# Two gate columns moved from plain products in the attention stage to a third seven-product unit in the recurrent stage

## The chip, the core and the metric

The program runs on one core of one Trainium2 chip, as a single launch. The metric is device time in microseconds (us). The engines are named as in the profile: PE (TensorE matmul), PEld (its weight load), DVE (VectorE), ACT (ScalarE), POOL (GpSimd) and SP (SyncE, which issues most of the DMAs).

## What is computed

The reference is one layer of a streaming encoder for 1024 prompt frames and 32 sample frames, of width 1024. What matters here is the first half of the layer: one input projection whose columns feed a windowed attention (A), a gated recurrence (B) and the two gates.

```python
h = _rms_norm(x, g_pre_mix)
z = h @ w_in
qa, ka, va, qb, fb, ib, ob, ga, gb = jnp.split(z, SPLIT_POINTS, axis=-1)
...
ya = _sink_attention(qblk, kblk, vblk, bias, mask, sinks)
yb, s_fin = _hgrn2(qb, fb, ib, s0, lb, block)
yb = _rms_norm(yb, g_hgrn_out) * jax.nn.silu(ob)
mix = jax.nn.sigmoid(ga) * (ya @ w_br_a) + jax.nn.sigmoid(gb) * (yb @ w_br_b)
x = x + _rms_norm(mix @ w_out, g_post_mix)
```

`ga` and `gb` are 1024 columns each. The kernel computes them in 16 blocks of 128 columns (called gate columns here, numbered 0 to 15 in the list `GATES`), takes their tanh and parks the result in DRAM until the branches are mixed.

## The kernel before

**Tokens and precision.** The 1056 frames lie across the free dimension in three groups of 384, 384 and 288 (`GR`). Each fp32 operand is held as a high part and a rest (`La`/`Lb` for the activations, `wh`/`wl` for a weight column, `wt` for both parts of a weight block), and each product is three matmuls: high by high, high by rest, rest by high.

**Plain columns.** `unit(out)` yields three blocks, one per token group. A block is 8 contraction steps of three matmuls, so 24 matmuls, issued in `product` (L205 to L207) in two halves of 12. One column is thus 72 matmuls. Its weights come through `load_next`: a DMA into a `wr` buffer, a cast on ACT (L184), and the rest either on DVE (L186) or, from the second attention pair on, by an ACT multiplication (L188) and an accumulating POOL DMA (L189). `gate_out` ends a gate block: tanh on ACT (L299), then a DMA to DRAM (L300).

**Attention stage.** Eight query columns hold two heads each ("pair" 0 to 7 here). For each pair nine score tiles are worked off: `scores` (PE L502 and L503, DVE L508, ACT L513, DVE L515 and L516, ACT L518), `turn` (PE transposes L539, then the split of the probabilities into `ph` on ACT L228 and `pl` on DVE L229) and `values` (PE L558 and L559, ACT L565, DVE L566 and L567). These small steps are put between the plain blocks of `blocks` by `stream`: those of pair `i` are spread over the three blocks of query column `i+1` and over `G_AT[i]` gate blocks. `G_AT` therefore says how many blocks of 24 matmuls stand beside each pair. Its sum over 3, `N_A`, is the number of gate columns done there. In pairs 1, 2, 4 and 5 `h_sums` adds sums of activations on DVE for the next stage (written to `t_d`).

**Between the stages.** One more plain gate column, `GATES[N_A]`, is streamed after the last pair, while the first weights of the next stage are prepared. The four sums are read back from `t_d` into `TL` (four DMAs, L991), and `t_split` makes `TH` (ACT L996) and the rest in `TL` (DVE L997).

**Recurrent stage.** Two weight columns at a time are multiplied by a Winograd form of Strassen's scheme: seven block products over the first two token groups (12 matmuls of 384 each), where plain products need eight, and four direct block products for the third group (12 matmuls of 288 each). `unit_pieces` (matmuls L1122, L1124, L1125) writes one such unit as 11 pieces. Its weights are loaded by `b_raw` (L1031) and summed and split by `b_parts` (L1043, L1044, L1049 to L1051, L1056). Each of the eight heads has two units, for (q, f) and (i, og). After the heads named in `G_AFTER`, a third unit holds two gate columns (`gate_unit`). `BU` lists all units in order; a unit's raw weights go to the two `wr` buffers or to two of the eight `wb` buffers in turn, counted from the end of `BU`, so that the last unit is in `wb`. The head's own work (`decay`, `factors`, `tile_in`, `tile_out`, `group_out`) is placed between the pieces by their number.

**After it.** Gate columns 14 and 15 are plain products again, and the branch products follow.

**Order.** What stands in the code is program order per step; a scheduler of the tile framework then fixes, at build time, one order per engine, and each engine works its own list in that order. `pinned` and `step` hold some steps behind others.

Of the kernel before, what the change touches and what calls it, by code (L numbers as in the profile page):

```python
# [59 lines left out]
def layer_kernel(  # L60
# [89 lines left out]

    plan = [in_cols(1024), in_cols(1152), in_cols(0)]
    GATES = [(ta_d[c], 5376 + c * P) for c in range(8)] + [(tb_d[c], 6400 + c * P) for c in range(8)]
    G_AT = (6,2,3,3,3,3,3,4)
    N_A = sum(G_AT) // 3
    plan_a = []
    for i in range(8):
        done, q = sum(G_AT[:i]), [("q", i + 1)] * (3 if i < 7 else 0)
        g = [("g", b // 3) for b in range(done, done + G_AT[i])]
        plan_a += g + q if i == 0 else q + g
# [120 lines left out]
    def unit(out):  # L280

        cell = []

        def get_w():
            if not cell:
                cell.append(next_w())
            return cell[0]
        return [(get_w, g, out) for g in range(3)]
# [6 lines left out]
    def gate_out(dst):  # L295
        def out(g, b):
            o, n = GR[g]
            t = gtile()
            S.activation(t[:, :n], b[:, :n], AF.Tanh, scale=0.5)  # L299
            dma(dst[:, o:o + n], t[:, :n])  # L300
        return out
# [17 lines left out]
    with right("ap") as ap:  # L319
# [93 lines left out]
        def q_out(i):  # L413
            def out(g, b):
                n = GR[g][1]
                qa = ap.tile([P, 384], F32R, tag="qa", name=nm("qa"), bufs=4)
                qb = ap.tile([P, 384], F32R, tag="qb", name=nm("qb"), bufs=4)
                if g == 2:
                    G.memset(qa[:, n + 32:384].bitcast(F32), 0.0)
                S.mul(qa[0:64, :n], b[0:64, :n], -0.125)  # L420
                V.scalar_tensor_tensor(qa[64:128, :n], b[0:64, :n], -0.125, qa[0:64, :n].bitcast(F32),
                                       op0=ALU.mult, op1=ALU.subtract)
                S.mul(qb[64:128, :n], b[64:128, :n], -0.125)
                V.scalar_tensor_tensor(qb[0:64, :n], b[64:128, :n], -0.125,
                                       qb[64:128, :n].bitcast(F32), op0=ALU.mult, op1=ALU.subtract)
                if g == 2:
                    G.tensor_copy(qa[:, n:n + 32], qb[:, SO:n].bitcast(F32))
                qs[i, g] = (qa, qb)
            return out
# [509 lines left out]
        for i in range(8):  # L939
            lo_ = 2 * len(blocks) if i else 0  # L940
            q = unit(q_out(i + 1)) if i < 7 else []
            g = [of_gates.pop(0) for _ in range(G_AT[i])]
            blocks += g + q if i == 0 else q + g
# [67 lines left out]
          5: (La[2][0:4], Lb[2][0:4]), 6: (La[2][4:8], Lb[2][4:8])}  # L1011


    G_AFTER = {3: N_A + 1, 7: N_A + 3}
    assert N_A + 5 == 14
    BU, unit_at = [], {}
    for h in range(8):
        unit_at[h] = len(BU)
        BU += [(1280 + h * P, 2304 + h * P), (3328 + h * P, 4352 + h * P)]
        if h in G_AFTER:  # L1020
            BU.append(tuple(GATES[G_AFTER[h] + a][1] for a in range(2)))
    NB = len(BU)
# [67 lines left out]
    with right("bp") as bp:  # L1090
# [121 lines left out]
        def gate_unit(h):  # L1212
            a, b = (gate_out(GATES[G_AFTER[h] + i][0]) for i in range(2))
            return unit_pieces(unit_at[h] + 2, lambda: gu, a,
                               lambda g: bt("x0", GMAX, 1)[:], b)
# [195 lines left out]
        for h in range(8):  # L1411
            m0 = len(pieces)
            pieces += qf_unit(h) + io_unit(h)
            m1 = m0 + NP
            if h in G_AFTER:
                pieces += gate_unit(h)
# [1510 lines left out]
def build(shapes):  # L2927
    import concourse.bacc as _bacc

    nc = _bacc.Bacc("TRN2", target_bir_lowering=False, num_devices=1)  # L2930
    args = [nc.dram_tensor(f"in_{n}_dram", s, F32, kind="ExternalInput").ap() for n, s in shapes]
    for i, shape in enumerate(_OUTS):
        args.append(nc.dram_tensor(f"out_{i}_dram", shape, F32, kind="ExternalOutput").ap())
    with tile.TileContext(nc) as tc:
        layer_kernel(tc, *args)
    return nc
# [10 lines left out]
```

## Time and profile before

| what | value |
|---|---|
| median of 3 runs | 1944.42 us (1942.07 to 1945.03) |
| the profiled execution | 1947.46 us |
| its span, first to last instruction | 1945.8 us |
| granted TensorE clock, mean over the span | 0.996 |
| busy share of the span | PE 99%, DVE 76%, ACT 53%, POOL 20% |
| attention pairs 1 to 7, with the column after them | about 112 us to 356 us of the span |
| recurrent stage | about 356 us to 825 us |

How to read it: "busy" is the time in which an instruction of the engine was under way, as the profiler models it. A matmul's own duration overlaps that of its neighbours, so the cost of a matmul in a dense stream is read from start to start, not from its duration. A row "X waited for Y" is idle time of engine X, and Y is what ended it. In a group's row, the last part is the idle time just before its instructions.

### The profile page before, as it was taken

How to read it: one execution, taken by the hardware profiler on the slowest of the kernel's cores; microseconds unless marked ns; L12 is line 12 of the kernel's file. 1: busy time of each engine (PE TensorE's matmuls, PEld its weight loads, DVE VectorE, ACT ScalarE, POOL GpSimd, SP SyncE). 2: the span in 40 equal slices, each digit the busy share in tenths (PEclk: the TensorE clock that was granted, in tenths of full speed). 3: DMA queues.
4: the chain of work that ended last, by engine and by line, in shares of the span. 5: the costliest groups of instructions: out<-in, count | busy, mean ns of one | idle time of the engine just before them, and what ended most of it. 6: DMA issues, size and time to landing. Idle time of an engine off the chain costs nothing.

```text
span 1945.8 us, 38169 instructions
## 1 busy us (share of the span) xinstructions
PE 1921.6 (99%) x14523; PEld 1903.9 (98%) x14523; DVE 1472.6 (76%) x3201; ACT 1028.7 (53%) x2214; POOL 381.4 (20%) x530
## 2 busy tenths in 40 slices
PE   8999999999999999999999999999999999999999
PEld 7999999999999999999999999999999999999998
DVE  5777777788888888755796878777787786768872
ACT  6667778666666666553445763333333336534432
POOL 2111211000101010132321113444644330000000
PEclk9999999999999999999999999999999999999999
DMA  8544443445547364498979684566897356755343
GB/s 267 150 111 129 127 131 90 149 114 139 146 106 162 118 122 101 129 312 272 293 203 296 230 280 131 161 171 188 158 187 183 115 186 215 220 178 159 117 131 88
DMA packets 319599, 329.11 MB, mean 169 GB/s; under 512 B 17432, under 2 KB 277435, under 8 KB 319416
## 3 DMA queue, kind: packets, MB, share of 16 engines
q1 hardware_dynamic: 274152, 218.92, 36.4%
q0 software_dynamic: 45136, 107.70, 23.1%
q8 instruction: 114, 1.87, 0.4%
q14 instruction: 69, 0.57, 0.1%
q10 hardware_dynamic: 128, 0.06, 0.0%
HBM read 234.48 MB, written 132.47 MB: 189 GB/s over the span
## 4 chain that ended last, share of the span: by engine, by line
PE 85%; DVE 6%; DMA 3%; ACT 3%; issue 2%; POOL 0%; SPq 0%; ACTq 0%; DVEq 0%; POOLq 0%
PE st L2373 7%; PE st L2372 7%; PE st L2371 7%; PE mm L205 4%; PE mm L206 4%; PE mm L207 4%; PE st L2499 4%; PE st L2501 4%; PE st L2500 4%; PE st L1663 2%; PE st L1665 2%; PE st L1667 2%; PE st L205 2%; PE st L206 2%; PE st L207 2%
## 5 line engine op out<-in xcount | busy, mean ns | idle before, releaser
L2373 PE MATMUL st<-op,wt 128*128 128x264 f32 x1232 | 349.9, 284 | 0.0
L2371 PE MATMUL st<-op,wt 128*128 128x264 f32 x1232 | 348.7, 283 | 1.2 <-ACT Sp L2383 0.5
L2372 PE MATMUL st<-op,wt 128*128 128x264 f32 x1232 | 347.8, 282 | 0.0
L2371 PEld LDWEIGHTS st<-op,wt 128*128 128x128 f32 x1232 | 231.3, 188 | 2.5 <-ACT Sp L2383 0.9
L2372 PEld LDWEIGHTS st<-op,wt 128*128 128x128 f32 x1232 | 231.5, 188 | 0.0
L2373 PEld LDWEIGHTS st<-op,wt 128*128 128x128 f32 x1232 | 230.9, 187 | 0.0
L2499 PE MATMUL st<-dop,wt 128*128 128x264 f32 x616 | 175.2, 285 | 2.6 <-ACT S L2514 2.6
L2501 PE MATMUL st<-dop,wt 128*128 128x264 f32 x616 | 175.0, 284 | 0.0
L2500 PE MATMUL st<-dop,wt 128*128 128x264 f32 x616 | 174.7, 284 | 0.0
L2030 ACT CAST wt<-wu 128x512 fp32r<-128x512 f32 x126 | 76.0, 618 | 176.4 <-POOL wu L2039 71.5
L205 PE MATMUL mm<-La,wh 128*128 128x384 f32 (+1 forms) x480 | 158.3, 330 | 0.0
L206 PE MATMUL mm<-Lb,wh 128*128 128x384 f32 (+1 forms) x480 | 155.2, 324 | 0.2 <-DVE Lb L784 0.2
L207 PE MATMUL mm<-La,wl 128*128 128x384 f32 (+1 forms) x480 | 155.0, 323 | 0.1
L2031 DVE TENSOR_TENSOR wt<-wu,wt 128x512 fp32r<-128x512 f32 x126 | 86.4, 694 | 46.0 <-ACT wt L2030 46.0
L2499 PEld LDWEIGHTS st<-dop,wt 128*128 128x128 f32 x616 | 116.3, 189 | 3.1 <-ACT S L2514 3.0
L2500 PEld LDWEIGHTS st<-dop,wt 128*128 128x128 f32 x616 | 116.5, 189 | 0.0
L2501 PEld LDWEIGHTS st<-dop,wt 128*128 128x128 f32 x616 | 116.2, 189 | 0.0
L2135 ACT CAST wt<-wd 128x512 fp32r<-128x512 f32 (+1 forms) x84 | 48.9, 586 | 90.8 <-PE st L2501 70.7
L206 PEld LDWEIGHTS mm<-Lb,wh 128*128 128x128 f32 x480 | 90.5, 189 | 0.8 <-DVE Lb L784 0.5
L207 PEld LDWEIGHTS mm<-La,wl 128*128 128x128 f32 x480 | 90.3, 188 | 0.5 <-DVE wl L759 0.5
L1122 PE MATMUL G<-La,wt 128*128 128x288 f32 x288 | 90.4, 314 | 0.0
L205 PEld LDWEIGHTS mm<-La,wh 128*128 128x128 f32 x480 | 90.4, 188 | 0.0
(628 smaller groups left out, 6328.2 us busy)
## 6 DMA issues: line engine op xcount, KB each, us to landing
wu<-in_w_up_dram SPq DMA_DIRECT2D x42, 512.0 KB
wu<-in_w_in_dram SPq DMA_DIRECT2D x36, 512.0 KB
w_d<-in_w_down_dram POOLq DMA_DIRECT2D x24, 704.0 KB, 8.4
a_d<-Up SPq DMA_DIRECT2D x21, 528.0 KB
wr<-in_w_in_dram SPq DMA_DIRECT2D x21, 512.0 KB
s_d<-sm SPq DMA_DIRECT2D x40, 264.0 KB
dop<-s_d SPq DMA_DIRECT2D x16, 528.0 KB
wr<-in_w_out_dram SPq DMA_DIRECT2D x16, 512.0 KB
```

The lines of the kernel that those rows point to most:

```text
L205: E.matmul(ps, wh, a, start=first and n == 0, stop=False)
L206: E.matmul(ps, wh, b, start=False, stop=False)
L207: E.matmul(ps, wl, a, start=False, stop=last and n == len(ks) - 1)
L1122: E.matmul(o, wh, x[0][k], start=first and k == 0, stop=False, skip_group_check=True)
L2030: S.copy(t[:, 0], src)
L2031: V.tensor_tensor(t[:, 1], src, t[:, 0].bitcast(F32), op=ALU.subtract)
L2371: E.matmul(o, wh, xh, start=first and k == 0, stop=False, skip_group_check=True)
L2372: E.matmul(o, wh, xl, start=False, stop=False, skip_group_check=True)
L2373: E.matmul(o, wl, xh, start=False, stop=k == 3, skip_group_check=True)
L2499: E.matmul(o, wh, xh_, start=first and k == 0, stop=False, skip_group_check=True)
L2500: E.matmul(o, wh, xl_, start=False, stop=False, skip_group_check=True)
L2501: E.matmul(o, wl, xh_, start=False, stop=k == ng - 1, skip_group_check=True)
```

## The change

`G_AT` goes from `(6,2,3,3,3,3,3,4)` (27 blocks, so `N_A` = 9) to `(5,2,2,2,2,2,3,3)` (21 blocks, `N_A` = 7). Pairs 0, 2, 3, 4, 5 and 7 lose one gate block each. Columns 0 to 6 are done beside the pairs, and column 7 instead of column 9 after the last pair. `G_AFTER` gets a third entry: columns 8 and 9 become a gate unit after head 1, columns 10 and 11 follow head 4 (before, head 3), and 12 and 13 follow head 7 as before. `BU` grows from 18 to 19 units, so the buffers that the units' raw weights alternate between are swapped for all units ahead of the added one.

```diff
-    G_AT = (6,2,3,3,3,3,3,4)
+    G_AT = (5, 2, 2, 2, 2, 2, 3, 3)
     N_A = sum(G_AT) // 3
...
-    G_AFTER = {3: N_A + 1, 7: N_A + 3}
-    assert N_A + 5 == 14
+    G_AFTER = {1: N_A + 1, 4: N_A + 3, 7: N_A + 5}
+    assert N_A + 7 == 14
```

The first place is PE in the last pair of the attention stage. `s` is a score tile, `sc` the softmax of one, `tr` and the `mm` of an L539 row a transposed tile, `o` the values, `ph` the probabilities; the L205 to L207 rows are a gate block. Before, from the last prompt score tile on:

```order
L503 MATMUL s_4646<-K_1_169,qb_4163 128x256
L207 MATMUL mm_4670<-La_157,wl_3942 128x384
L205 MATMUL mm_4670<-La_157,wh_3941 128x384
L478 MATMUL s_4661<-K_1_167,qa_4162 128x160
L479 MATMUL s_4661<-K_1_169,qa_4162 128x160
L206 MATMUL mm_4670<-Lb_161,wh_3941 128x384
L539 MATMUL tr_4639<-ident,sc_4473 128x128 x4
L207 MATMUL mm_4670<-La_157,wl_3942 128x384
L205 MATMUL mm_4670<-La_157,wh_3941 128x384
L206 MATMUL mm_4670<-Lb_161,wh_3941 128x384
L207 MATMUL mm_4670<-La_157,wl_3942 128x384
L539 MATMUL tr_4685<-ident,sc_4510 128x128 x4
```

Now, 14 matmuls of a gate block behind the same score tile (here `s_4411`, with the softmax `sc_4416`):

```order
L539 MATMUL tr_4509<-ident,sc_4319 128x128 x4
L207 MATMUL mm_4534<-La_536,wl_3775 128x288
L205 MATMUL mm_4534<-La_536,wh_3774 128x288
L539 MATMUL tr_4518<-ident,sc_4334 128x128 x4
L539 MATMUL mm_4567<-ident,sc_4416 128x128
L206 MATMUL mm_4534<-Lb_538,wh_3774 128x288
L207 MATMUL mm_4534<-La_536,wl_3775 128x288
L539 MATMUL mm_4567<-ident,sc_4416 128x128 x3
L558 MATMUL o_4596<-ph_4491,Vs 128x256
L559 MATMUL o_4596<-pl_4492,Vs 128x256
L539 MATMUL tr_4549<-ident,sc_4386 128x128 x4
L533 MATMUL mm_4576<-ident,sc_792 128x128 x2
```

Before, the transposes of the pair's tiles stand apart, with gate matmuls and other tiles' values between them. Now five of them stand within a few rows, and the one of the last prompt score tile comes after 19 gate matmuls of 288 columns, 2 of the sample's scores and two sets of 4 transposes.

The second place is SP between the stages. `ya` is a finished pair, `nt` its negated half, `gt` a gate block, `TL` the four sums, `wu` the raw weights of a recurrent unit. Before:

```order
L569 DMA ya_d<-ya_4428 512x1x264
L300 DMA tb_d_96<-gt_4896 128x384
L991 DMA TL_4849<-t_d_123 128x1536
L991 DMA TL_4852<-t_d_124 128x1536
L991 DMA TL_4855<-t_d_125 128x1536
L991 DMA TL_4858<-t_d_126 128x1536
L300 DMA tb_d_96<-gt_4927 128x384
L300 DMA tb_d_96<-gt_4959 128x288
L1031 DMA wu_5021<-in_w_in_dram 128x8x128
L1031 DMA wu_5023<-in_w_in_dram 128x8x128
```

Now:

```order
L569 DMA ya_d<-ya_4274 512x1x264
L300 DMA ta_d_94<-gt_4745 128x384
L991 DMA TL_4667<-t_d_123 128x1536
L991 DMA TL_4670<-t_d_124 128x1536
L991 DMA TL_4673<-t_d_125 128x1536
L991 DMA TL_4676<-t_d_126 128x1536
L300 DMA ta_d_94<-gt_4777 128x288
L1031 DMA wu_5061<-in_w_in_dram 128x8x128
L1031 DMA wu_5063<-in_w_in_dram 128x8x128
```

The four `TL` loads still stand behind the last pair's `ya` and one gate block. But the `gt` ahead of them is now the second block of the column after the last pair (before, its first), and the `wu` loads behind them are those of the third unit: the weights of the first and second unit (`wu_4691`, `wu_4693`, `wu_4839`, `wu_4841`) are all issued well ahead of this place, beside the last pairs, where before the second unit's (`wu_5021`, `wu_5023`) stood behind `TL`. On all engines the order from the last head's end to the end of the program is the same in both.

## The prediction

> **What bounds the kernel now.** First the page: the span, the engines' shares and the chain that ended last.
>
> ```profile
> span 1945.8 us, 38169 instructions
> PE 1921.6 (99%) x14523; PEld 1903.9 (98%) x14523; DVE 1472.6 (76%) x3201; ACT 1028.7 (53%) x2214; POOL 381.4 (20%) x530
> PE 85%; DVE 6%; DMA 3%; ACT 3%; issue 2%; POOL 0%; SPq 0%; ACTq 0%; DVEq 0%; POOLq 0%
> ```
>
> PE is the bound by its share and by the chain. A share is an average, so next the waits of PE alone, in the two stages that the change touches. Columns: time in all, times, longest. The attention pairs from 66 to 345 us, then the hand-over and the recurrent stage from 345 to 845 us:
>
> ```profile
> PE tr L539 <- DVE pl L229: 0.6, 3, 0.2
> PE s L502 <- DVE st L508: 0.4, 2, 0.2
> ```
>
> ```profile
> PE Y L1122 <- DVE vt L1143: 0.6, 1, 0.6
> ```
>
> In 780 us PE stood still for 1.6 us. So the time of both stages is PE's list of work, and a change there is worth the PE work that it removes, as long as the cover holds. Whether it holds is read from the other engines' busy time per stretch: pairs 1, 2 and 4, most of pair 7, and the recurrent stage.
>
> ```profile
> core 0: us, PE busy (x) PEld busy (x) DVE busy (x) ACT busy (x) POOL busy (x), PEclk, DMA share, GB/s
> 112.00:142.30 30.30, 30.30 (x213) 30.19 (x212) 24.79 (x81) 22.95 (x67) 6.37 (x16) 1.00 0.45 123
> 142.30:177.50 35.20, 35.08 (x248) 34.50 (x246) 28.36 (x93) 26.99 (x73) 7.02 (x19) 1.00 0.48 130
> 212.10:247.10 35.00, 34.81 (x247) 34.48 (x245) 27.11 (x85) 26.17 (x71) 7.25 (x19) 1.00 0.43 118
> 316.20:338.00 21.80, 21.14 (x152) 20.22 (x151) 16.61 (x66) 18.20 (x57) 2.91 (x12) 1.00 0.25 64
> 380.00:820.00 440.00, 439.41 (x2936) 437.03 (x2935) 371.59 (x1040) 280.63 (x730) 44.65 (x80) 1.00 0.51 125
> ```
>
> The first row is the most useful one. Pair 1 already has the two gate blocks that pairs 2 to 5 get by the change, it carries `h_sums` too, and PE is busy for all of its 30.30 us.
>
> **The PE work.** Start to start in the clean stretch at the hand-over, the five rows begin a 384-wide block, a 288-wide block, a 384-wide piece, a 288-wide piece and the next piece:
>
> ```profile
> 348.50 0.33 PE L205 MATMUL mm<-La,wh 128*128 128x384 f32 x1
> 352.66 0.29 PE L205 MATMUL mm<-La,wh 128*128 128x288 f32 x1
> 355.85 0.34 PE L1122 MATMUL X<-La,wt 128*128 128x384 f32 x1
> 357.93 0.29 PE L1122 MATMUL G<-La,wt 128*128 128x288 f32 x1
> 359.52 0.34 PE L1122 MATMUL Y<-TH,wt 128*128 128x384 f32 x1
> ```
>
> A block of 24 matmuls of 384 columns takes 4.16 us (173 ns each), one of 288 takes 3.19 us (133 ns); the pieces of 12 take 2.08 and 1.59 us. A plain column is 2 × 4.16 + 3.19 = 11.51 us, two are 23.02 us. A unit is 7 × 2.08 + 4 × 1.59 = 20.92 us. The change takes away the first and adds the second: **-2.1 us**. The head's and the pairs' own PE work is the same in number. The Trainium skill, "TensorE: Matmul & The Clock Gate", section "Back-to-back issue gap", gives N / 2.4 + 2.5 ns per isolated matmul, 162.5 and 122.5 ns here; by it the difference would be 1.95 us. The trace shows about 11 ns more per matmul, so the rows are used.
>
> **What the new unit asks of the others.** Its splits and evacuations are priced by the groups of the existing units:
>
> ```profile
> L1044 DVE TENSOR_TENSOR wt<-wu,wt 128x512 fp32r<-128x512 f32 x108 | 72.7, 684 | 16.5 <-ACT wt L1043 15.9
> L1043 ACT CAST wt<-wu 128x512 fp32r<-128x512 f32 x108 | 65.1, 618 | 47.8 <-DVE wu L1051 23.8 <-DVE wt L1044 13.2 <-PE G L1125 7.6
> L299 ACT ACTIVATE gt<-mm 128x384 f32<-128x384 f32 (+1 forms) x30 | 13.6, 454 | 5.1 <-issue 3.2 <-PE mm L207 1.7
> ```
>
> DVE: 8 splits and 4 sums at 0.68, 5 subtractions of about 0.55 (estimated from 512 columns at 0.68): 10.9 us. ACT: 8 casts at 0.62, a copy and 6 tanh at about 0.45: 8.1 us. Against 20.92 us of PE that is 52% and 39%, below the stage's own 84% (371.59 of 440) and 64%. So the unit adds slack to the recurrent stage, and I cost it at nothing beside PE. If PE's cover failed there, the most is a few stalls like the one of 0.6 us above. Its two `wu` loads replace two `wr` loads of the same 512 KB; the two POOL accumulations of the plain columns go, and with them 2 casts, 2 multiplications and 6 tanh of ACT in the attention stage, none of which PE waited for.
>
> **The pairs.** Pairs 2 to 5 become like pair 1, about 31 us for 35. The fullest is pair 2: DVE 28.36 us of work. It has 2.6 us left in 31, where pair 1 has 5.5; pair 4 has 3.9. PE does not wait in pair 1, and pair 3 has no `h_sums`, so a backlog can drain there. I take 0 for pairs 0 to 6 (0 to +0.7).
>
> **The last pair** is different. It drops a 288 block, 3.19 us of 21.8, and had the only waits of the stage besides. The rows show its last prompt score tile: scores done, then the two halves of its softmax.
>
> ```profile
> 329.86 0.28 PE L503 MATMUL s<-K,qb 128*128 128x256 f32 x1
> 335.19 0.33 DVE L516 TENSOR_SCALAR sc<-sc,st 128x256 f32<-128x256 f32 x1
> 335.04 0.51 ACT L518 ACTIVATE sc<-sc,st 128x256 f32<-128x256 f32 x1
> ```
>
> From 330.14 to 335.55 it took 5.4 us. In the changed order PE has 19 gate matmuls of 288 (2.5 us), two of scores and 8 transposes (about 1 us, estimated from the 0.28 us rows) between: 3.5 us. If the queues are as full as now, 1.9 us is missing; if they are empty, nothing. Five tiles are transposed there within a few rows through two `tr` banks and the `mm` banks, each needing a cast and a subtraction of about 0.6 us before its bank is free. I take **+1.2 us** beyond the present 0.66 (21.80 less 21.14), with ends of -0.6 (all waits gone) and +3.2 (the whole block bare).
>
> **The first weight cast** of the recurrent stage now stands in ACT's list ahead of the last pair's softmax, and waits for a `wu` load issued when the last query block is done. Three gate blocks (11.5 us) lie between, against a load of 7.82 us (below), so it costs nothing. A late load would hold the last pair's exponentials one for one.
>
> **The hand-over.** The chain there, from the last values to the first use of `TL`:
>
> ```profile
> 345.59 0.12 PE o L559
> 348.70 0.50 ACT gt L299
> 349.65 6.53 DMA TL<-t_d
> 356.26 0.84 ACT TH L996
> 357.12 0.71 DVE TL L997
> 357.84 7.82 DMA wu<-in_w_in_dram
> ```
>
> Before, PE had 13.9 us of other work from 345.6 to 359.52, and the first half of `TL` was ready at 357.84, so 1.7 us early. Now the order leaves 14 matmuls of 384 and 24 of 288 of the plain column, then 21 of 384 and 12 of 288 of the first unit: 2.4 + 3.2 + 3.6 + 1.6 = 10.8 us. The load is issued after a gate block that ends 2.4 us behind the last values (2.9 before), so all is ready after 2.4 + 1.15 + 6.53 + 1.66 = 11.7 us. The first matmul that needs the split half has a few others ahead of it, at about 11.7 us too. It is a tie: **+0.4 us** (0 to +2.0, when the second and third loads, which follow, are late as well). On the other side, the second unit's weights no longer stand behind `TL` in SP's queue: the wait of 0.6 us in that unit may go. I take half: **-0.3 us**.
>
> **The sum**, made against this execution (span 1945.8 us, 1947.46 us in all, 3.04 above the median of three) and applied to the median: -2.1 + 1.2 + 0.4 - 0.3 = -0.8. 1944.42 - 0.8 is **1943.6 us**. About 0.2%, 3.9 us, is what a measurement here tells from no change.
>
> **Rivals.** *Full cover.* The last pair and the hand-over add nothing, and the 0.6 us goes: -2.7, 1941.7 us. For it: 780 us with 1.6 us of waits, so the scheduler's order has held so far. Against it: the last pair's waits stand where the cover is cut now. Still within 0.2%.
>
> *The end of the attention stage is bare.* The last pair loses all 3.2 us and the hand-over 3.1 (13.9 less 10.8): -2.1 + 6.3 = +4.2, 1948.6 us. It decides when a tile's softmax keeps its 5.4 us while its cover falls to 3.5, for several tiles in turn, and `TL` lands later than 6.5 us.
>
> *The softmax chain sets the pace of the full pairs* (slower). Place: pairs 2, 4 and 5, where `h_sums` fills DVE. If such a pair cannot run in less than its present 35 us, the dropped block (11.51 / 3 = 3.8 us) comes back as a wait each time: -2.1 + 11.5, 1953.8 us. It decides once DVE work plus unavoidable gaps pass 31 us; pair 2 needs 28.4 plus gaps. Pair 1 at 30.30 us without a wait speaks against it. The Trainium skill, "Perfetto Trace Analysis", section "Optimization Strategy", says of kernels whose bound changes over time that "performance may be improved by interleaving those regimes". The change separates PE-heavy columns from the stage with the softmax, so by that rule this rival is the way to go; the first window row, PE busy for 30.30 of 30.30, is so far against it.
>
> **Chances.** The forecast 0.55 (its own range 1942 to 1946), full cover 0.27, the bare end 0.08, the full pairs 0.05, and 0.05 for a gain that no row shows. From these: faster by over 0.2% 0.05, within it 0.84 (forecast, full cover, and a little of the bare end), slower 0.11. The range: low, -2.1 with every wait of both places gone (-0.6, -0.6) and 0.4 of the spread of the runs, 1940.7; high, -2.1 + 3.2 + 2.0 + 0.7, 1948.2. The full pairs and about half of the bare end lie above it.
>
> **What would show it.** Right: pairs 2 to 5 take 30 to 31.5 us with PE idle under 0.3 us each; L539 and L502 wait 1 to 3 us in all in the last pair, on DVE L229 and L508; at most 1 us at the first L1122 `Y<-TH`; no new wait at the gate units after heads 1 and 4; the rest of the program as long as before. Wrong: pairs near 35 us, a PE wait on ACT L1043 or on a `wu` load in the last pair, or waits of PE in the recurrent stage of more than 2 us.

## The result and the profile after

The changed kernel takes **1953.88 us** (median of 7 runs, 1950.10 to 1958.95), the kernel before 1944.40 us (7 runs, 1942.07 to 1945.78). The ratio is 1.0046, with a 95% interval of 1.0034 to 1.0058: slower by some 9 us, where 0.8 us faster was forecast. The runs of the changed kernel also lie further apart. The profiled execution took 1958.95 us and is the longest of the seven, so its trace shows the loss at its largest.

Page of the changed kernel: the span, PE's share and the chain that ended last.

```profile
span 1957.2 us, 38174 instructions
PE 1925.4 (98%) x14511; PEld 1902.2 (97%) x14511; DVE 1483.4 (76%) x3218; ACT 1028.9 (53%) x2219; POOL 381.0 (19%) x528
PE 72%; DVE 5%; DMA 3%; ACT 2%; issue 2%; POOL 0%; SPq 0%; DVEq 0%; ACTq 0%; POOLq 0%
```

PE is still the bound. Its waits in the same two stretches as before, the pairs from 66 to 345 us and then the recurrent stage to 845 us:

```profile
PE mm L205 <- DVE pl L229: 3.0, 2, 2.7
PE s L502 <- DVE st L508: 1.7, 3, 0.9
PE tr L539 <- DVE pl L229: 0.8, 3, 0.3
```

```profile
PE tr L1302 <- DVE dec L1288: 0.7, 1, 0.7
PE Y L1122 <- ACT TH L996: 0.7, 1, 0.7
PE Y L1122 <- DVE vt L1143: 0.3, 1, 0.3
```

The pairs now have 5.5 us of waits (1.0 before), the recurrent stage 1.7 (0.6). Where the time went shows in the stretches from one sample score tile (first matmul at L478) to the next, here with the gate blocks that the change takes out of each, a block being 3.84 us on average, a third of a plain column. Stretch 0 begins with the first score tile, 7b ends with the first product of the recurrent stage:

| stretch | 0 | 1 | 2 | 3 | 4 | 5 | 6 | 7 | 7b |
|---|---|---|---|---|---|---|---|---|---|
| before, us | 46.9 | 30.7 | 34.8 | 35.0 | 35.0 | 34.9 | 34.7 | 19.7 | 25.5 |
| blocks taken out | 1 | 0 | 1 | 1 | 1 | 1 | 0 | 0 | 1 |
| after, us | 44.2 | 30.6 | 31.3 | **34.4** | 30.9 | 31.7 | **39.2** | 19.9 | 22.0 |
| lost beside the blocks | 1.1 | -0.1 | 0.3 | **3.2** | -0.3 | 0.6 | **4.5** | 0.2 | 0.3 |

So the pairs that carry `h_sums` and lost a block (2, 4, 5) came out at 30.9 to 31.7 us, close to the 30 to 31.5 that the prediction gave. The loss is in pair 3, which has no `h_sums`, and in pair 6, whose number of blocks did not even change. Pair 0 adds 1.1 us, most of it a wait of PE at L385 (1.3 us, 0.4 before).

PE at the start of pair 6: the last row before its longest wait, and the first rows behind it.

```profile
269.53 0.28 PE L503 MATMUL s<-K,qb 128*128 128x256 f32 x1
272.52 0.69 PE L205 MATMUL mm<-La,wh 128*128 128x384 f32 x1 [2.71 <-DVE pl L229]
273.00 0.53 PE L206 MATMUL mm<-Lb,wh 128*128 128x384 f32 x1
273.32 0.53 PE L207 MATMUL mm<-La,wl 128*128 128x384 f32 x1
273.64 0.53 PE L205 MATMUL mm<-La,wh 128*128 128x384 f32 x1
```

The gate block waits for a PSUM bank that DVE frees at L229. DVE's subtraction waits for ACT's `ph`, and ACT, in the same stretch, stood still ahead of it (its last two rows here are what DVE waits for):

```profile
262.51 0.44 ACT L573 ACTIVATE nt<-ya 128x264 f32<-128x264 f32 x1
...
266.56 1.06 ACT L188 ACTIVATE wl<-wr 128x1024 fp32r<-128x1024 f32 x1
269.95 0.42 ACT L573 ACTIVATE nt<-ya 128x264 f32<-128x264 f32 x1 [2.34 <-DMA sa_d<-nt]
270.28 0.57 ACT L565 COPY u<-o 128x512 f32<-128x512 f32 x1
270.75 0.59 ACT L228 CAST ph<-mm 128x512 fp32r<-128x512 f32 x1
```

`nt` is the negated half of `ya` that `values` makes after a pair's last tile (L571 to L575) and copies to `sa_d`. It has no buffer of its own: its two halves take `hs0` and `hs1`, two of the four buffers of `h_sums`, and there is only one buffer of each name. The `nt` of pairs 0, 1, 3 and 4 has to wait until the sums of the next pair have left those buffers. So the `nt` of pair 4 is made late, its second half at 262.51 us (first row above), and that of pair 5, with no sums between, comes 7 us behind and needs the same buffer. SyncE's queue in that stretch (start and length of each issue), after and then, in the like place, before:

```profile
260.81 0.32 SPq L575 DMA_DIRECT2D sa_d<-nt x1
261.29 2.21 SPq L453 DMA_DIRECT2D bias<-rb_d x2
264.40 0.38 SPq L1031 DMA_DIRECT2D wu<-in_w_in_dram x1
264.88 1.14 SPq L575 DMA_DIRECT2D sa_d<-nt x1
270.40 0.31 SPq L575 DMA_DIRECT2D sa_d<-nt x1
```

```profile
271.25 0.39 SPq L175 DMA_DIRECT2D wr<-in_w_in_dram x1
273.10 0.90 SPq L575 DMA_DIRECT2D sa_d<-nt x2
279.77 0.38 SPq L1031 DMA_DIRECT2D wu<-in_w_in_dram x1
280.26 1.31 SPq L453 DMA_DIRECT2D bias<-rb_d x2
```

Before, both copies of a pair are issued together, ahead of the bias and weight loads. With a block less in the pair, the scheduler's order puts the bias loads and a weight load between them, and the second copy is issued at 264.88; ACT goes on at 269.95, 5 us later. At the end of pair 2 the same happens with 3.56 us. The groups of L573, with what ended ACT's idle time before it, before and after:

```profile
L573 ACT ACTIVATE nt<-ya x16: 418/425/429, 135.2 to 347.5; 128x264 f32<-128x264 f32 x16
  DVE ya L567: 2.4, 5
  DMA t_d<-hs: 1.2, 3
```

```profile
L573 ACT ACTIVATE nt<-ya x16: 416/425/445, 132.6 to 338.0; 128x264 f32<-128x264 f32 x16
  DMA sa_d<-nt: 5.9, 2
  DVE ya L567: 1.8, 3
```

The 5.9 us are new. Last, the granted clock, stretch by stretch around the wait (columns: the stretch, its length, then PE, PEld, DVE, ACT and POOL busy, then clock, DMA share and GB/s):

```profile
268.97:272.38 3.41, 0.84 (x7) 0.64 (x5) 1.45 (x4) 1.38 (x3) 1.19 (x3) 1.00 0.76 165
272.38:275.80 3.42, 3.28 (x10) 3.29 (x11) 2.56 (x12) 2.36 (x9) 0.00 (x0) 0.50 0.53 132
275.80:279.21 3.41, 3.41 (x25) 3.41 (x25) 2.35 (x9) 2.63 (x8) 0.00 (x0) 1.00 0.34 103
```

Behind the wait the clock was 0.50 for 3.42 us: matmuls of 384 stand 0.32 us apart (273.00, 273.32, 273.64) instead of 0.173. Eleven of them cost 1.6 us on top of the 2.71.

The recurrent stage took 491.1 us from its first to its last product, 467.8 before: 23.3 us more, 2.4 beyond the 20.92 of the unit's own work. First and last starts of two of its products, before and after:

```profile
L1122 PE MATMUL X<-La,wt x144: 333/334/473, 355.8 to 803.7; 128*128 128x384 f32 x144
L1122 PE MATMUL G<-La,wt x288: 288/295/432, 357.9 to 820.7; 128*128 128x288 f32 x144
```

```profile
L1122 PE MATMUL X<-La,wt x152: 334/334/473, 341.7 to 812.9; 128*128 128x384 f32 x152
L1122 PE MATMUL G<-La,wt x304: 288/294/431, 343.8 to 829.9; 128*128 128x288 f32 x152
```

The account of the profiled execution against that of before: up to the first score tile -1.1, attention stage -13.1 (297.4 to 284.3) where -23.0 was expected, recurrent stage +23.3, the rest +2.2: together the 11.4 us between the spans, to a tenth. The rest, behind the recurrent stage, is not touched by the change or by any experiment below, and takes 1118.6 to 1124.4 us in the traces of this case. So what one trace has more than another is compared by stage here, not by span.

### The profile page after: what moved, and what is told of

Its sections match the earlier page's. It is cut to its first block, busy times and chain, and to the rows that moved or that the text cites. A ratio compares the mean times of both kernels' runs of the same rounds, so it can differ in the third digit from the quotient of the medians.

```text
span 1957.2 us, 38174 instructions
## 1 busy us (share of the span) xinstructions
PE 1925.4 (98%) x14511; PEld 1902.2 (97%) x14511; DVE 1483.4 (76%) x3218; ACT 1028.9 (53%) x2219; POOL 381.0 (19%) x528
## 3 DMA queue, kind: packets, MB, share of 16 engines
q8 instruction: 114, 1.87, 0.4%
## 4 chain that ended last, share of the span: by engine, by line
PE 72%; DVE 5%; DMA 3%; ACT 2%; issue 2%; POOL 0%; SPq 0%; DVEq 0%; ACTq 0%; POOLq 0%
PE st L2373 7%; PE st L2371 7%; PE st L2372 7%; PE st L2499 4%; PE st L2501 4%; PE st L2500 3%; PE st L205 2%; PE st L206 2%; PE Y L1122 2%; PE st L207 2%; PE Y L1125 2%; PE Y L1124 2%; PE G L1122 2%; PE G L1125 2%; PE G L1124 2%; DMA wa<-wa_d 2%
## 5 line engine op out<-in xcount | busy, mean ns | idle before, releaser
L2499 PE MATMUL st<-dop,wt 128*128 128x264 f32 x616 | 175.2, 285 | 3.1 <-ACT S L2514 3.1
L2030 ACT CAST wt<-wu 128x512 fp32r<-128x512 f32 x126 | 76.0, 618 | 176.3 <-POOL wu L2039 71.4
L205 PE MATMUL mm<-La,wh 128*128 128x384 f32 (+1 forms) x432 | 142.9, 331 | 3.0 <-DVE pl L229 3.0
L206 PE MATMUL mm<-Lb,wh 128*128 128x384 f32 (+1 forms) x432 | 140.5, 326 | 0.6 <-DVE Lb L784 0.6
L207 PE MATMUL mm<-La,wl 128*128 128x384 f32 (+1 forms) x432 | 140.1, 325 | 0.1
L2031 DVE TENSOR_TENSOR wt<-wu,wt 128x512 fp32r<-128x512 f32 x126 | 86.4, 694 | 46.0 <-ACT wt L2030 46.0
L2499 PEld LDWEIGHTS st<-dop,wt 128*128 128x128 f32 x616 | 116.4, 189 | 3.8 <-ACT S L2514 3.7
L1122 PE MATMUL G<-La,wt 128*128 128x288 f32 x304 | 95.2, 313 | 0.0
L1043 ACT CAST wt<-wu 128x512 fp32r<-128x512 f32 x114 | 68.5, 617 | 50.2 <-DVE wu L1051 19.7
L1044 DVE TENSOR_TENSOR wt<-wu,wt 128x512 fp32r<-128x512 f32 x114 | 77.0, 686 | 18.3 <-ACT wt L1043 17.3
L1124 PE MATMUL G<-Lb,wt 128*128 128x288 f32 x304 | 89.9, 296 | 0.0
```

The lines of the kernel that those rows point to most:

```text
L205: E.matmul(ps, wh, a, start=first and n == 0, stop=False)
L206: E.matmul(ps, wh, b, start=False, stop=False)
L207: E.matmul(ps, wl, a, start=False, stop=last and n == len(ks) - 1)
L1122: E.matmul(o, wh, x[0][k], start=first and k == 0, stop=False, skip_group_check=True)
L1124: E.matmul(o, wh, x[1][k], start=False, stop=False, skip_group_check=True)
L2031: V.tensor_tensor(t[:, 1], src, t[:, 0].bitcast(F32), op=ALU.subtract)
```

## The experiments

**Theory 1.** ACT works its list in order. At the ends of pairs 2 and 5 it stands still at L573 for a staging buffer that a late copy still holds; the casts and exponentials behind it come late, and PE runs dry in pairs 3 and 6. **Rival 2.** With a block less, the softmax chain on DVE and ACT sets the pace of the pairs. **Rival 3.** The third gate unit costs the recurrent stage far more than its work.

### Other buffers for two pairs

```diff
-nt = aq.tile([P, GMAX], F32, tag=f"hs{p}", name=nm("nt"), bufs=1)
+nt = aq.tile([P, GMAX], F32, tag=f"hs{p + 2 * (i in (2, 5))}", name=nm("nt"), bufs=1)
```

PE's, DVE's, POOL's and SyncE's lists stay as they were, word for word; ACT's changes by one row's place and by its waits.

> The changed kernel, with one edit: the two staging tiles nt of pairs 2 and 5 take the buffers hs2 and hs3 instead of hs0 and hs1, so that the negation at L573 of those pairs no longer waits until pair 1's and pair 4's copies have left hs0 and hs1. Theory 1 (ACT stands still at L573 behind that transfer, 3.56 us at 175 and 2.34 us at 270, and TensorE runs dry behind it): both waits go, the pair from 163.5 to 197.9 comes down from 34.4 to 31-32 us, the one from 260.6 to 299.8 from 39.2 to 35-36 us, and the median from 1953.9 to 1945-1948, with a scatter as small as before's 4 us. Rival 2 (with one gate block less per pair the softmax chain on DVE and ACT sets the pace): no change, 1952-1955. Rival 3 (the loss comes from the third gate unit in the recurrence): no change, 1952-1955.

Measured: 1948.45 us (9 runs, 1946.76 to 1951.48), ratio to before 1.0025 (1.0015 to 1.0035). L573's group in this kernel:

```profile
L573 ACT ACTIVATE nt<-ya x16: 417/426/448, 132.7 to 332.3; 128x264 f32<-128x264 f32 x16
  DVE ya L567: 2.2, 4
  DMA t_d<-hs: 0.5, 1
```

The waits on the copies are gone, stretch 3 takes 32.0 us (34.4 without the edit) and stretch 6 35.9 (39.2). Each median held against that of the kernel before run beside it (1943.57 us here), the change cost 9.5 us and now costs 4.9. Rivals 2 and 3 said no change. But some 5 us stay, more than theory 1 allowed: its 1948 is passed by half a us.

The same edit in the kernel before:

> The kernel before, with the same edit on the staging tiles. Its trace shows no wait of L573 for the copies (3.6 us in all, for DVE's ya and for the hs transfers). Theory 1: within 1.5 us of before, 1943-1946. If the edit itself brings several us whatever the kernel, theory 1 is not what sets after apart from before. Rivals 2 and 3: no change.

Measured: 1943.96 us (11 runs), ratio 1.0004 (0.9995 to 1.0013). The edit by itself brings nothing.

### The wait put into the kernel before

```diff
-nt = aq.tile([P, GMAX], F32, tag=f"hs{p}", name=nm("nt"), bufs=1)
+nt = aq.tile([P, GMAX], F32, tag="hs0", name=nm("nt"), bufs=1)
```

> The kernel before, with the suspected wait put in: both staging tiles nt of every pair use the one buffer hs0, so that the second negation of a pair must wait until the first one's copies have left it (2 to 7 us from the negation to the landing in the traces so far). Blocks, units and TensorE's order are those of before. Theory 1 (ACT standing still at L573 runs TensorE dry): L573 shows new waits on sa_d<-nt of 4 to 15 us in all, and the time rises by 3 to 10 us, to 1947-1954. Rivals 2 and 3 (pace of the chain, third unit): within 1.5 us of before.

Measured: 1950.84 us (5 runs, 1949.50 to 1953.16), ratio 1.0036 (1.0023 to 1.0048). L573's group, and the two longest of PE's waits from 100 to 300 us:

```profile
L573 ACT ACTIVATE nt<-ya x16: 421/425/427, 134.6 to 354.8; 128x264 f32<-128x264 f32 x16
  DMA sa_d<-nt: 16.4, 5
```

```profile
PE o L558 <- ACT sc L513: 3.0, 1, 3.0
PE tr L539 <- DVE pl L229: 1.5, 2, 1.3
```

With all its blocks, its two units and PE's list unchanged (the other engines' lists differ in a few places), the kernel before loses 7 us when ACT has to wait for the copies, somewhat longer than the 4 to 15 us expected. That shows the mechanism from the other side. Of 16.4 us of standing still, about 7 reach the end: PE has other work for the rest.

### The copies through GpSimd's queue

```diff
-dma(sa_d[q][:, p, i % 4], nt[:, :H])
+(gdma if i in (1, 4) else dma)(sa_d[q][:, p, i % 4], nt[:, :H])
```

> The changed kernel, with the copies sa_d<-nt of pairs 1 and 4 issued on GpSimd's queue instead of SyncE's, where they stand behind 2 bias loads (1.73 and 2.21 us of issue) and a weight load (0.48 and 0.38 us). The buffers stay shared. Theory 1 in the form that the place in SyncE's queue makes the copy late: the waits at L573 fall from 3.56 and 2.34 us to under 1.5 each, and the time to 1946-1950. Theory 1 in the form that the transfer itself is slow among the others (5.0 us from issue to landing, DMA share 0.95): the waits fall by at most the 2 us of issue and the time stays at 1950-1954. Rivals 2 and 3: no change, 1952-1955.

Measured: 1951.24 us (5 runs, 1949.26 to 1955.51), ratio 1.0042 (1.0027 to 1.0058). ACT's wait for `sa_d<-nt` falls from 5.9 to 2.7 us in all, PE's wait in pair 6 from 2.71 to 2.30:

```profile
269.18 0.45 PE L205 MATMUL mm<-La,wh 128*128 128x384 f32 x1 [2.30 <-DVE pl L229]
```

About half of ACT's wait came from the place in SyncE's queue, the other half is there without it, while the DMA engines are full (share 0.95 from 262 to 266 us in this trace as in that of the changed kernel). The two pairs differ: the wait at the end of pair 2 falls from 3.56 to 0.82 us, and stretch 3 takes 32.0 us as with the other buffers, so there the queue was the main part; the one at the end of pair 5 falls only from 2.34 to 1.91, and stretch 6 still takes 37.3. In the time of all runs the two forms can't be told apart: the interval overlaps that of the change.

### The third unit alone

In the kernel before, the third unit computes columns 7 and 8 a second time, so there is one unit's work too much.

```diff
-G_AFTER = {3: N_A + 1, 7: N_A + 3}
+G_AFTER = {1: 7, 4: N_A + 1, 7: N_A + 3}
```

> The kernel before, with all its nine plain columns, and a third gate unit beside the heads 1, 4 and 7 that computes two columns (7 and 8) a second time: the recurrence of the changed kernel with the attention of before, and 20.92 us of TensorE work too much. Theory 1: before plus 20.9 and at most 2.5 for the recurrence's new small waits, 1965-1968. Rival 3 (the third unit costs some 9 us beyond its work): 1973-1976.

Measured: 1968.99 us (4 runs, 1967.62 to 1970.50), ratio 1.0130 (1.0116 to 1.0143), so 25 us more, with an interval of 22.5 to 28. Rival 3 falls, but the result lies 1 us above what theory 1 gave. In this trace the recurrent stage takes 489.8 us, 22.0 more than before: 1.1 beyond the work. The two traces differ by 22.7 us in all; that the medians differ by 25 goes with the traced execution of before, which took 3.0 us more than the median then.

### Other heads, other buffers for the units

Both with the staging tiles swapped as above, and the units beside other heads:

```diff
-G_AFTER = {1: N_A + 1, 4: N_A + 3, 7: N_A + 5}
+G_AFTER = {3: N_A + 1, 5: N_A + 3, 7: N_A + 5}
```

> The changed kernel with the staging tiles swapped, and the three gate units beside the heads 3, 5 and 7 instead of 1, 4 and 7. If part of the loss is a head without a unit behind it (the recurrence took 2.3 us more than the unit's work; 0.90 us of it a new stop of TensorE before L1302 at head 3, which had a unit in before): that stop goes, 1947-1948. If a unit costs the same wherever it stands: 1948.5, within 0.5.

```diff
-G_AFTER = {1: N_A + 1, 4: N_A + 3, 7: N_A + 5}
+G_AFTER = {0: N_A + 1, 3: N_A + 3, 7: N_A + 5}
```

> The changed kernel with the staging tiles swapped, and the three gate units beside the heads 0, 3 and 7. If the stops at the start of the recurrence (0.28, 0.14 and 0.33 us within the first head) and the one before L1302 are what the recurrence loses: both go, 1946.5-1947.5. If a unit costs the same wherever it stands: 1948.5, within 0.5. If the unit at head 0 makes its weights' preparation on DVE and ACT late at the hand-over: 1949-1951, with a new stop in the first 40 us of the recurrence.

Measured: 1947.88 and 1948.34 us (11 runs each), both at a ratio of 1.0020 (1.0011 or 1.0010 to 1.0029). The heads make no difference, and the wait of 0.74 us before L1302 is there in both. Then the exchange of the two kinds of weight buffers, undone:

```diff
-odd = (NB - u) % 2
+odd = (NB + 1 - u) % 2
```

> The changed kernel with the staging tiles swapped, and the two kinds of buffers for the units' raw weights (wr and wb) exchanged, so that unit 0 of the recurrence takes the kind that it has in before; with 19 units instead of 18 the change had exchanged them. In before each of the two gate units lengthens its head by 20.8-20.9 us, in all kernels with three the first one by 22.0 (a wait of 0.74 before L1302 at its start) and the others by 20.8, whichever heads they stand at. If the exchanged buffers make the first one late: that wait goes, the recurrence comes from 491.0 down to 490, and the time to 1947-1948. If not: 491 and 1948.5.

Measured: 1946.89 us (11 runs), ratio 1.0013 (1.0005 to 1.0022), the recurrent stage 491.0 us as without the edit. The wait is not gone, it has moved to the second gate unit. Put together by the buffers that a unit's raw weights take, from the starts of the transposes at L1302, where a head without a gate unit takes 53.6 to 53.7 us:

| gate unit's raw weights in | units | its head takes | so the unit costs |
|---|---|---|---|
| `wr` | before: after head 3; all kernels with three: one of the first two | 74.5 us | 20.8 us |
| `wb` | all kernels with three: the other one (the first; the second here) | 75.5 us | 21.9 us |

So the expectation named the right parts, but which unit is late depends on its own buffers, not on the exchange as such. With three units one of those in the middle is always in `wb`. That is 1.1 us. The unit after head 7 ends the stage and can't be read in this way. Why `wb` makes a unit late wasn't tried.

### Where the blocks are taken out

With the staging tiles swapped, two other tables.

```diff
-G_AT = (5, 2, 2, 2, 2, 2, 3, 3)
+G_AT = (2, 2, 3, 3, 3, 3, 2, 3)
```

> The changed kernel with the staging tiles of the first run swapped as there, and the six gate blocks taken out elsewhere: G_AT = (2, 2, 3, 3, 3, 3, 2, 3) instead of (5, 2, 2, 2, 2, 2, 3, 3), so that pairs 1 to 5 keep the gate blocks of before, pair 0 gives up four, and pairs 6 and 7 one each. If what is left of the loss in the attention (about 2.5 us, small waits at the scores and transposes of the pairs with two gate blocks, and one of 0.85 at 267) comes from shortening the middle pairs: 1945-1947.5. If pair 0, whose casts of keys and values share ACT and DVE, runs dry instead: 1949-1953. If the place makes no difference: 1948-1949.

```diff
-G_AT = (5, 2, 2, 2, 2, 2, 3, 3)
+G_AT = (5, 2, 2, 2, 2, 3, 2, 3)
```

> The changed kernel with the staging tiles swapped, and pair 5 keeping its third gate block while pair 6 gives one up: G_AT = (5, 2, 2, 2, 2, 3, 2, 3). With the swap alone the stretch of pair 6 took 35.9 us for 34.7 before, and pair 5 31.7 for 34.9 less a block of 3.84 (31.1). If that loss hangs on a short pair 5 (whose end then brings the staging copies, the bias loads and the weight casts together): pairs 5 and 6 take 65.9 us instead of 67.6, and the time 1946.5-1947.5. If any shortened pair costs 0.3 to 0.8 wherever it is: 1948-1949.

Measured: 1950.69 us (7 runs, ratio 1.0033, 1.0022 to 1.0044) and 1947.84 us (12 runs, 1.0024, 1.0012 to 1.0036). In the first, stretch 0 takes 34.5 us, 3.0 more than 46.9 less four blocks: pair 0 runs dry. In the second, stretches 5 and 6 take 66.4 us instead of 67.6, between the two expectations, and so does the time. The traced execution of the second lost 3.8 us at another place: at 746.76 us, in the recurrent stage, PE waited 2.12 us for DVE (L1208) and then ran at half clock. Taking the blocks from elsewhere brings nothing that can be measured.

### The negation off ACT

With the staging tiles swapped, GpSimd negates:

```diff
-S.mul(nt[:, :H], ya[:, o:o + H], -1.0)
+G.tensor_scalar(nt[:, :H], ya[:, o:o + H], -1.0, None, op0=ALU.mult)
```

> The changed kernel with the staging tiles swapped, and the negation into them made by GpSimd instead of ACT, so that no transfer out of a staging tile can hold up ACT's list at all (about 0.5 us of waiting for the hs transfers and 2 us for ya are left in it with the swap alone), and 16 ACT instructions of 0.43 us go. Theory 1: as good as the swap alone or better, 1946-1948.5. If GpSimd now stands still and with it the copies of the sinks into sc that the scores wait for: slower than the swap alone, 1949-1953, with new waits for POOL before L508.

Measured: 1952.78 us (6 runs, 1951.64 to 1960.24), ratio 1.0051 (1.0036 to 1.0066). Slower, but not where the expectation looked. The attention stage takes 275.1 us, 22.3 less than before, with stretches 3 and 6 at 31.5 and 34.7: nothing is left there of the loss. All of it comes behind, at the hand-over. PE's longest wait from 330 us on:

```profile
PE Y L1122 <- ACT TH L996: 5.8, 1, 5.8
```

GpSimd's list around the last negation, with SyncE's `TL` loads, in this kernel:

```profile
327.42 0.87 POOL L573 TENSOR_SCALAR nt<-ya 128x264 f32<-128x264 f32 x1 [4.98 <-issue]
329.25 0.97 POOL L1452 DMA_DIRECT2D sa_d<-ya_d x1 [0.16 <-issue]
330.24 3.00 SPq L991 DMA_DIRECT2D TL<-t_d x4
```

The last two in the kernel with the swap alone:

```profile
319.45 0.95 POOL L1452 DMA_DIRECT2D sa_d<-ya_d x1 [0.35 <-DMA ya_d<-ya]
335.07 2.87 SPq L991 DMA_DIRECT2D TL<-t_d x4
```

The first product of the recurrent stage starts at 331.18 us here and at 336.00 with the swap alone. So the `TL` loads are issued equally early in both, 0.9 us ahead of it, and SyncE is not late. But `TH`, which needs the first of them, starts 10.8 us behind the first issue here and 5.7 there. What differs is the copy of 1056 KB at L1452: in GpSimd's list it now stands behind the negation of pair 7, and is issued 1.9 us ahead of the first product instead of 16.6, together with the `TL` loads, while the DMA engines are full (share 0.95 or more from 331 to 341 us). That the copy takes the loads' share of the DMA engines is inferred from this. If GpSimd makes `nt` for pairs 0 to 5 only, and ACT keeps pairs 6 and 7, the copy no longer stands behind a negation:

```diff
-S.mul(nt[:, :H], ya[:, o:o + H], -1.0)
+if i < 6:
+    G.tensor_scalar(nt[:, :H], ya[:, o:o + H], -1.0, None, op0=ALU.mult)
+else:
+    S.mul(nt[:, :H], ya[:, o:o + H], -1.0)
```

> The changed kernel with the staging tiles swapped, and the negation on GpSimd for pairs 0 to 5 only; pairs 6 and 7 keep it on ACT, so that SyncE's queue does not stand behind them at the hand-over. Theory 1: the attention is 275 us as with GpSimd throughout (297.5 in before), the wait of 5.8 us at the first Y<-TH is below 0.7 again, the recurrence 490 to 491 (467.8 in before), so 0 to 1.5 us over before: 1944-1946. If the hand-over stays late or the middle pairs lose again: 1948 or more.

> The kernel before with both of these edits (swapped tiles, the negation on GpSimd for pairs 0 to 5). Theory 1: its ACT hardly waited at L573, so it changes by less than 1.5 us, 1942.5-1945, and the change itself, the difference to the other run, is worth 0 to 2 us to the worse: the 23.0 us that leave the attention come back in the recurrence as 20.9 of work, 1.1 for a gate unit in the wb buffers and 1 at the hand-over.

Measured: 1946.56 us (12 runs, 1942.63 to 1950.89; ratio 1.0012, 1.0002 to 1.0022) for the changed kernel, 1943.08 us (12 runs; ratio 0.9996, 0.9988 to 1.0005) for the kernel before. The attention stage takes 275.6 us against 297.1 (-21.5), the recurrent stage 490.8 against 467.7 (+23.1). The copy at L1452 (L1455 in this kernel) is again issued 16.6 us ahead of the first product, and the wait at the first `Y<-TH` is 0.4 us. The expectation put that wait down to SyncE's queue; the edit was right, the reason was not. No form of the change has a lower median, though the one with the buffer kinds exchanged (1946.89) can't be told from it. With the same edits the kernel before is still 3.5 us faster by the medians, more than the 0 to 2 expected. The two stages hold 1.6 us of it; the rest is not located, and runs of one kernel differ by more: the two traced executions took 1944.15 and 1944.43 us.

## Why the prediction was wrong, step by step

**The PE work (-2.1)** was right in its own terms. A unit costs 20.8 us where nothing is late, and with ACT's way free the attention stage gives back 21.5 to 22.3 of the 23.0 us.

**Pairs 0 to 6 (0, at most +0.7)** is the step that failed: some 9 us in the profiled execution, the slowest of the seven. Its argument was that pair 1, with two blocks, runs without a wait, that DVE has room, and that "pair 3 has no `h_sums`, so a backlog can drain there". The room was there: pairs 1, 2, 4 and 5 took 30.6 to 31.7 us. But room by busy time says nothing of a single wait in an in-order list. The missing `h_sums` in pairs 3 and 6 is just what brings two pairs' staging copies together: the first set is held up to the end of the pair with sums, the second is not. The order of SyncE's and ACT's lists in pairs 3 and 6 was not read, only that of the last pair and the hand-over. Shown: the wait at L573 (the swap takes 4.6 us off the medians' 9.5, the same kind of wait put into before adds 7). The rest in these pairs, waits of 0.2 to 0.9 us, goes when the negation leaves ACT.

**The last pair (+1.2)** took 41.9 us with the column behind it, for 45.2 less a block of 3.19 to 3.84: it lost nothing, to half a us. **The hand-over (+0.4)** came out at +0.9 to 1.3 us in the first head of the recurrent stage (34.2 to 34.6 us, 33.3 before): the tie was lost, within the bounds given. **The second unit's wait (-0.3)** fell from 0.6 to 0.3. **The first weight cast (0)** made no wait.

**The new unit beside PE (0)** was too low by 1.1 us. The prediction compared DVE's and ACT's sums of work with PE's. The exchange of `wr` and `wb` was seen and not priced.

**The rivals.** The one on the full pairs gave 1953.8 us, the time that was measured, and was still wrong: it put the loss into pairs 2, 4 and 5 through DVE's work, and these ran at 31 us. A time that fits is no proof of its mechanism; the stretches tell them apart. The Trainium skill, "Perfetto Trace Analysis", section "Optimization Strategy", advises interleaving regimes. The sign of the result agrees with it, but not the place: the pairs of that rival ran at 31 us. The same section goes on to what would have helped here: find what the engine's gaps wait for, and take a gap that repeats on the engine that should be busy as a hint that there are too few buffers for the next tile. The loss here stands in two stretches of nine, hardly a gap that repeats, but its cause is of that kind: ACT's waits at L573, 5.9 us for two buffers with two users.

**What stays open.** Some 2 us between the medians of the changed kernel and of before, both with the last edits; the reason why a unit in `wb` is late; and how much of the copies' delay is queue and how much transfer.

## What to carry to other kernels

When a move shortens the work beside a chain, read the in-order lists of every engine at each stage's end, and of each tile with one buffer ask who had it last and which transfer must land first: a free engine by its busy time can still stand still for a buffer. A pair that is not edited can take the loss (here pair 6), so compare all stretches, not only the changed ones. And price a move with the cover as it would be at its best: here even that gave nothing, 21.5 us saved for 23.1 paid.

## What the hardware showed beside

Short waits of PE were followed by half clock in some cases and not in others. Which ones shows when a trace is cut into steps of 3.41 us: within each trace, the changes to half clock and back lie whole numbers of such steps apart. The windows below are such steps: two in the kernel before, around a wait of 1.90 us at L2499, and two in the changed kernel with swapped staging tiles, around a wait of 2.92 us at L1663.

```profile
1620.04:1623.45 3.41, 1.51 (x12) 1.30 (x12) 2.10 (x4) 3.41 (x7) 0.54 (x1) 1.00 0.43 162
1623.45:1626.87 3.42, 3.42 (x18) 3.42 (x17) 3.10 (x5) 2.68 (x6) 0.00 (x0) 0.50 0.50 151
```

```profile
911.29:914.70 3.41, 2.08 (x18) 1.87 (x16) 0.00 (x0) 0.52 (x1) 0.00 (x0) 1.00 1.04 351
914.70:918.11 3.41, 1.82 (x15) 1.85 (x16) 3.11 (x5) 1.34 (x3) 0.20 (x1) 1.00 0.12 36
```

The 1.90 us lie within one step, and the next step runs at 0.50. The 2.92 us fall on two steps, 1.33 us of idle time in one and 1.59 in the other, and the clock stays at 1.00. Of the 2.71 us in pair 6, 2.57 us lie in one step (0.84 of 3.41 busy, above), and the next ran at 0.50. In the 15 traces of this case, without the first 40 and the last 8 us, 16 steps have PE idle for 1.81 us or more; 15 of them were followed by a step at half clock, one (1.87 us) was not. No step with 1.79 us or less was. So it counts how much of a wait falls into one step, and that differs from run to run. A half-clock step with PE busy costs 1.7 us; the trace of the changed kernel has three, that with the swapped tiles none, that of before two, so they move a run's time by some us, which is about the spread of the runs here. That they make the spread was not tried. The Trainium skill, "TensorE: Matmul & The Clock Gate", section "What's actually happening", says that the clock halves after an idle window of about 3.4 us that runs freely, and comes back after as long a busy one. The window's length and the return agree (3.41 us). That all of it must be idle does not: 1.81 us of idle time in a step was enough.
